# A token-major value projection in one pass of 512 columns over four PSUM banks

## The chip, the cores and the metric

The kernel runs on one core of one Trainium2 chip. Its engines work side by side, each through its own list of instructions in order: PE (TensorE, matmuls into PSUM; PEld is its weight load), DVE (VectorE), ACT (ScalarE), POOL (GpSimd) and SP (SyncE, which issues nearly all transfers). The metric is device time in microseconds (us) of one execution; lower is better. Before the change it is 1659.42 us, the median of 3 runs.

## The reference

Two layers of a decoder trunk over 512 tokens of width 2048, in float32. Each layer normalises its input, makes one wide projection of it, runs four mixers on slices of that (a gated linear attention GLA, a gated recurrence LRU, a sparse attention NSA and a convolution module, the Conformer), gates and merges them, and projects back:

```
def hybrid_layer(x, ...):
    h = rmsnorm(x, pre_g)
    proj = h @ w_in
    (gla_q, gla_k, gla_v, ..., conv_z) = jnp.split(proj, ...)
    o_a = gla_mixer(gla_q, gla_k, gla_v, ...)      # also lru, nsa, conformer
    mixed = jnp.concatenate([o_a, o_b, o_c, o_d], axis=-1)
    y = (group_rmsnorm(mixed, branch_g) * silu(z)) @ w_out
    return x + rmsnorm(y, post_g)
```

The change concerns gla_v alone: 512 tokens x 512 columns, a product over 2048 input features.

## The kernel before

Each float32 operand is split in two parts, hi and lo, of a shorter format; a product is three matmuls that add up in one PSUM bank (mm3, L198): hi x hi, hi x lo, lo x hi. The normalised input lies in SBUF as 16 feature tiles H[kk], L[kk] of 128 features x 512 tokens. Weights come in units of 128 x 1024 numbers (unit, L155): one transfer into a raw buffer (2 of them), then two splits of 512 columns each, hi by ACT (L144) and lo by DVE or POOL (L145), into whi and wlo (5 buffers each, N_W).

PSUM has eight banks of 128 x 512 float32. Four of them (pool acc) belong to the projections, three (mx) to the mixers' short products, one (op) to longer ones. Most projections (proj, L248) have the weights as stationary operand and fill one acc bank with 128 output columns x 512 tokens (tile pfm); the copy out of it, by `scaled` (L261) or a multiply, frees the bank. The value projection has tokens on the partitions instead: H is stationary and the weights move, so one bank holds 128 tokens, and four blocks of tokens b make the whole. It is done in two passes of 256 columns (loop hf): in each, two banks hold two blocks of tokens each, and for each of 16 feature tiles and each b three matmuls of 256 columns run. Eight units of weights serve a layer, four per pass. At the end of a pass ACT copies the four blocks into gv (L881). The tm projection (L795) before it is of the same kind, with four banks and 284 columns.

The mixers' work is a list of tasks, Python generators that emit a little at a time; `advance(budget)` runs them between projections, `flush` runs them out. The order that each engine gets is made from this by the tile scheduler at build time. It goes by priorities: matmuls of projections are in the band "last", so they fill PE where nothing else is ready, and loads, splits and copies of projections are in the band "first".

Around the value projection these are at work, in program order:
- `conformer_tail` (L365): the pointwise product pw_ps, then group_norm (L265) of four tiles: square (L270), split, a sum over channels in a bank gn_ps (chan_sum), root (ACT L204) and reciprocal (DVE L205), then a multiply that writes yconf.
- `compress` (L410): for each of kc and vc (tile kv) four units. A unit adds a position term to a slice of kv (L424), into one of the four slots of a ring, pbuf; splits that into zc (L426, L427); loads 128 x 1024 weights into mraw (one buffer), splits them into mhi and mlo (one buffer each, L144, L145), and adds 16 matmuls into the bank ch_ps. Behind the four units of kc, ACT copies ch_ps to the next ring slot (L438), and the matmul cf_ps reads it.
- `queries(0)` (L842) projects two NSA query heads before GLA's q and k (qk) are projected. Its two pfm banks are copied into q (L263).

Two lines say where kv and q lie: tiles with one tag share one buffer, so q can be written only after the last read of kv.

```
kvt = self.quad("t4", "kv")        # L826
qt = self.quad("t4", "q")          # L852
```

Of the kernel before, what the change touches and what calls it, by code (L numbers as in the profile page):

```python
# [13 lines left out]
AF = mybir.ActivationFunctionType  # L14
# [7 lines left out]
P = 128  # L22
KT = D // P
# [3 lines left out]
GLA_Q, GLA_K, GLA_V, GLA_FG, GLA_Z = 0, 256, 512, 1024, 1040  # L27
# [11 lines left out]
GV_UNIT = 8 + 2 * len(FM_TILES)  # L39
# [22 lines left out]
class Trunk:  # L62
# [649 lines left out]
    def layer(self, l, xs):  # L712
        nc, a, dve, act, gp = self.nc, self.a, self.dve, self.act, self.gp
        STEP = BUDGET
        STEP_N, STEP_Z = BUDGET_N, BUDGET_Z
# [8 lines left out]
        first = [self.bank(f"f{i}", self.acc, "acc") for i in range(4)]  # L724
# [7 lines left out]
        units = {}  # L732
        for u, t in steps:
# [7 lines left out]
            for k in (2 * u, 2 * u + 1):  # L741
                if l == 0:
                    self.put_h(H, L, k, self.x_of(xs, k), self.col(V_PRE + k))
                hi, lo = units[u][k % 2]
                with self.band("last"):
                    for i in range(4):
                        w = slice(i * P, (i + 1) * P)
                        self.mm3(first[i][:, tok], hi[:, w], lo[:, w], H[k][:, tok], L[k][:, tok],
                                 k == 0 and t == 0, k == KT - 1 and t == len(halves) - 1,
                                 skip_group_check=len(halves) > 1)  # L750
# [10 lines left out]
        rtok = self.rstd(sums, range(4), True)  # L761
# [34 lines left out]
        for kk in range(KT):  # L796
            if kk % 2 == 0:
                parts = self.unit(a["w_tm"][l, kk // 2], 2 * TM, TM)
            hi, lo = parts[kk % 2]
            with self.band("last"):  # L800
                for b in range(4):
                    tb = slice(b * P, (b + 1) * P)
# [9 lines left out]
        for b in range(4):  # L812
            with self.band("first"):
                act(tm[b], ptm[b][:, :TM], AF.Copy, scale=rtok[:, 2 * b:2 * b + 1])
            w = slice(b * 256, b * 256 + 256)
# [43 lines left out]
                    self.stt(qk[:, (2 * p + i) * 512:(2 * p + i + 1) * 512], ps, s, self.rbc, ALU.mult, ALU.mult)  # L859
                self.advance(STEP_N)  # L860
        gv = self.quad("t6", "gv")
        for hf in range(2):
            pv = [self.bank(f"gv{i}", self.acc, "acc") for i in range(2)]
            for u in range(4):
                parts = self.unit(a["w_in"][l, GV_UNIT + 4 * hf + u])
                with self.band("last"):
                    for k in range(4):
                        kk = 4 * u + k
                        hi, lo = parts[k // 2]
                        w = slice(k % 2 * 256, (k % 2 + 1) * 256)  # L870
                        for b in range(4):
                            tb = slice(b * P, (b + 1) * P)
                            o = pv[b // 2][:, (b % 2) * 256:(b % 2) * 256 + 256]
                            self.mm3(o, H[kk][:, tb], L[kk][:, tb], hi[:, w], lo[:, w],
                                     kk == 0 and b % 2 == 0, kk == KT - 1 and b % 2 == 1, skip_group_check=True)
                if u % 2 == 1:
                    self.advance(STEP_N)
            for i in range(2):
                for b in (2 * i, 2 * i + 1):
                    with self.band("first"):  # L880
                        act(gv[:, 512 * b + 256 * hf:512 * b + 256 * hf + 256],  # L881
                            pv[i][:, (b % 2) * 256:(b % 2) * 256 + 256], AF.Copy, scale=rtok[:, 2 * b:2 * b + 1])
        self.flush()
        queries(1, qt[:, 1024:])
        self.tasks.append(self.group_norm(NSA))
# [53 lines left out]
        o = [self.quad(f"t{i}", "o") for i in range(4)]  # L939
# [6 lines left out]
        H, L = self.nextH or (None, None)  # L946
# [25 lines left out]
def lay_out(x, pre_norm_g, w_in, gla_w_fg2, gla_b_fg2, lru_conv_w, lru_conv_b, lru_w_a, lru_b_a, lru_w_x, lru_b_x,  # L972
            lru_lambda, nsa_cmp_pos_k, nsa_cmp_w1_k, nsa_cmp_w2_k, nsa_cmp_pos_v, nsa_cmp_w1_v, nsa_cmp_w2_v,
            conf_dw_w, conf_dw_b, conf_ln_g, conf_ln_b, conf_pw_w, conf_pw_b, branch_norm_g, w_out, post_norm_g):
    n = DEPTH
    d = {}
    d["xT"] = np.ascontiguousarray(np.asarray(x)[0].T).reshape(4, 4, P, S).transpose(0, 2, 1, 3)
    w = np.asarray(w_in).reshape(n, KT, P, -1)

    def block(k0, k1, cols):  # L980
        b = w[:, k0:k1][..., cols]
        return b.transpose(0, 2, 1, 3).reshape(n, P, -1)

    units = []
    first = np.concatenate([np.arange(c, c + P) for c in FIRST4])
    for u in range(8):
        units.append(block(2 * u, 2 * u + 2, first))
    for c in FM_TILES:
        for h in range(2):
            units.append(block(8 * h, 8 * h + 8, np.arange(c, c + P)))  # L990
    for hf in range(2):
        for u in range(4):
            units.append(block(4 * u, 4 * u + 4, np.arange(GLA_V + 256 * hf, GLA_V + 256 * hf + 256)))
    d["w_in"] = np.stack(units, axis=1)
    tmc = np.concatenate([np.arange(NSA_VS, NSA_VS + P), np.arange(NSA_VW, NSA_VW + P),
                          np.arange(NSA_G, NSA_G + 12), np.arange(GLA_FG, GLA_FG + 16)])
    d["w_tm"] = np.stack([block(k, k + 2, tmc) for k in range(0, KT, 2)], axis=1)
    wo = np.asarray(w_out).reshape(n, KT, P, KT, P)[:, ORDER].reshape(n, 2, 8, P, KT, P)
    d["w_out"] = np.ascontiguousarray(wo.transpose(0, 4, 1, 3, 2, 5)).reshape(n, 2 * KT, P, 1024)

    def cols(t, m):
        return np.asarray(t).reshape(n, m, P).transpose(0, 2, 1)

    def taps(t):
        t = np.asarray(t)
        return t.reshape(n, t.shape[1], 4, P).transpose(0, 3, 2, 1).reshape(n, P, -1)

    d["vec"] = np.concatenate(
        [cols(pre_norm_g, 16), cols(post_norm_g, 16), cols(branch_norm_g, 16)[:, :, ORDER], taps(lru_conv_w), cols(lru_conv_b, 4),
         cols(lru_b_a, 4), cols(lru_b_x, 4), cols(lru_lambda, 4), taps(conf_dw_w), cols(conf_dw_b, 4),  # L1010
         cols(conf_ln_g, 4), cols(conf_ln_b, 4), cols(conf_pw_b, 4), cols(gla_b_fg2, 2)], axis=2)
    d["lru_w"] = np.concatenate([np.asarray(t).transpose(0, 2, 1, 3).reshape(n, P, 512) for t in (lru_w_a, lru_w_x)], axis=2)
    d["pw_w"] = np.asarray(conf_pw_w).reshape(n, 2, 2, P, 512).transpose(0, 1, 3, 2, 4).reshape(n, 2, P, 1024)
    d["w_fg2"] = np.repeat(np.pad(np.asarray(gla_w_fg2), ((0, 0), (0, 16), (0, 0)))[:, None], 3, axis=1).reshape(n, 96, 256)
    d["cmp_pos"] = np.concatenate([np.asarray(t).transpose(0, 2, 1) for t in (nsa_cmp_pos_k, nsa_cmp_pos_v)], axis=2)
    d["cmp_w2"] = np.concatenate([np.asarray(nsa_cmp_w2_k), np.asarray(nsa_cmp_w2_v)], axis=2)
    d["cmp_w1"] = np.stack([np.asarray(t).reshape(n, 4, 8, P, P).transpose(0, 1, 3, 2, 4).reshape(n, 4, P, 1024)
                            for t in (nsa_cmp_w1_k, nsa_cmp_w1_v)], axis=1)
    con = np.zeros((P, NCON), np.float32)
    i = np.arange(P)  # L1020
    con[:, C_ID:C_ID + P] = np.eye(P)
    con[:, C_TRI + 128:C_TRI + 256] = np.where(i[None, :] <= i[:, None], 0.0, NEG)
    t = np.arange(4)[None, :, None] * P + i[:, None, None]
    con[:, C_CMP:C_CMP + 124] = np.where(t >= 16 * np.arange(31)[None, None] + 31, 0.0, NEG).reshape(P, 124)
    con[:, C_GLA:C_GLA + P] = (i[:, None] // 64 == i[None] // 64) & (i[:, None] <= i[None])
    con[:62, C_FOLD:C_FOLD + 31] = np.concatenate([np.eye(31), np.eye(31)])
    d["consts"] = con
    return {k: np.ascontiguousarray(t) for k, t in d.items()}
# [18 lines left out]
```

## Time and profile before

| | |
|---|---|
| median of 3 runs | 1659.42 us (1657.36 to 1660.86) |
| the profiled execution | 1658.41 us, its span 1656.6 us |
| PE busy | 1600.3 us, 8380 matmuls |
| DVE / ACT / POOL busy | 1025.5 / 728.3 / 515.3 us |
| mean granted TensorE clock | 0.988 |
| value projection, layer 0 / 1 | starts at 301.26 / 1122.71 us |

The span runs from the first to the last instruction. Times within it count from its start. A matmul's duration reaches into the next one's, so the pace of PE is read from the starts. In a row of a timeline the bracket at the end is the idle time of that engine before the instruction and what ended it.

### The profile page before, as it was taken

The page shows a single profiled execution, that of the slowest core. Times are in us where ns is not written, and L with a number is a line of the kernel's source. Part 1 is how long each engine was busy: PE and PEld are TensorE (multiplying, and loading weights), DVE is VectorE, ACT ScalarE, POOL GpSimd, SP SyncE. Part 2 cuts the span into 40 slices and gives each one's busy share as a digit, 9 for nine tenths or more (in the row PEclk, how much of TensorE's full clock was granted, in tenths as well). Part 3 has the DMA queues.
Part 4 walks back from the last instruction along what each step waited for, and adds up shares of the span by engine and source line. Part 5 has one row for each costly group of instructions (what it writes and reads, how often), then busy time and mean ns, then how long its engine had stood idle before and what let it go on. Part 6 is the DMA issues. An engine that isn't in the chain of part 4 may idle for free.

```text
span 1656.6 us, 22323 instructions
## 1 busy us (share of the span) xinstructions
PE 1600.3 (97%) x8380; PEld 1356.3 (82%) x8380; DVE 1025.5 (62%) x1630; ACT 728.3 (44%) x1307; POOL 515.3 (31%) x431
## 2 busy tenths in 40 slices
PE   7999989999999998999999999999999999999996
PEld 6889878998888777888888898779988887778886
DVE  8488978554666758111396888876546757581115
ACT  6322463544456625333353234545444456353331
POOL 1354262121122422222245543521211234132224
PEclk9999999999999999999999999999999999999998
DMA  7322322242112223333343223222521121333323
GB/s 246 103 91 81 114 76 90 90 148 98 52 65 92 77 92 118 121 102 98 98 142 108 97 88 100 78 96 84 165 78 39 64 79 64 140 115 102 100 91 115
DMA packets 53708, 165.53 MB, mean 100 GB/s; under 512 B 5792, under 2 KB 14688, under 8 KB 52576
## 3 DMA queue, kind: packets, MB, share of 16 engines
q1 hardware_dynamic: 52224, 162.79, 29.9%
q8 instruction: 66, 1.08, 0.3%
q10 hardware_dynamic: 1376, 1.31, 0.2%
q14 instruction: 42, 0.34, 0.1%
HBM read 155.69 MB, written 8.39 MB: 99 GB/s over the span
## 4 chain that ended last, share of the span: by engine, by line
PE 81%; DVE 11%; ACT 4%; issue 3%; DMA 1%; POOL 0%; SPq 0%; DVEq 0%; ACTq 0%; POOLq 0%
PE pfm L196 39%; PE out_ps L196 19%; PE gv L196 6%; PE tm L196 3%; PE f L196 2%; PE o_ps L196 2%; DVE wlo L145 2%; PE s_ps L196 2%; PE pw_ps L196 1%; DVE L L131 1%; DVE gn_ps L205 1%; PE pt_ps L529 1%; PE go_ps L196 1%; PE ch_ps L196 1%; DVE o L691 1%
## 5 line engine op out<-in xcount | busy, mean ns | idle before, releaser
L144 ACT ACTIVATE whi<-raw 128x512 fp32r<-128x512 f32 (+1 forms) x512 | 313.0, 616 | 626.3 <-PE pfm L196 293.4
L145 POOL TENSOR_TENSOR wlo<-raw,whi 128x512 fp32r<-128x512 f32 (+1 forms) x229 | 294.0, 1285 | 836.2 <-ACT whi L144 755.0
L196 PE MATMUL pfm<-H,whi 128*128 128x512 f32 x1152 | 453.9, 394 | 0.0
L196 PE MATMUL pfm<-L,whi 128*128 128x512 f32 x1152 | 453.2, 393 | 0.0
L196 PE MATMUL pfm<-H,wlo 128*128 128x512 f32 x1152 | 452.5, 393 | 0.0
L145 DVE TENSOR_TENSOR wlo<-raw,whi 128x512 fp32r<-128x512 f32 x283 | 223.4, 794 | 322.1 <-ACT whi L144 320.9
L196 PEld LDWEIGHTS pfm<-H,whi 128*128 128x128 f32 x1152 | 217.6, 189 | 46.3 <-issue 1.2
L196 PEld LDWEIGHTS pfm<-H,wlo 128*128 128x128 f32 x1152 | 217.6, 189 | 45.4 <-issue 0.3
L196 PEld LDWEIGHTS pfm<-L,whi 128*128 128x128 f32 x1152 | 217.4, 189 | 45.5 <-issue 0.9
L196 PE MATMUL out_ps<-H,wlo 128*128 128x512 f32 (+1 forms) x576 | 211.3, 367 | 5.3 <-DVE wlo L145 5.3
L196 PE MATMUL out_ps<-L,whi 128*128 128x512 f32 (+1 forms) x576 | 210.9, 367 | 1.0 <-DVE L L233 1.0
L196 PE MATMUL out_ps<-H,whi 128*128 128x512 f32 (+1 forms) x576 | 209.8, 367 | 0.0
L131 DVE SCALAR_TENSOR_TENSOR cv_ps<-yv,vec,cv_ps 128x512 f32<-128x512 f32 x232 | 175.1, 755 | 7.2
L196 PEld LDWEIGHTS out_ps<-H,wlo 128*128 128x128 f32 x576 | 108.9, 189 | 24.0 <-DVE wlo L145 6.6
L196 PEld LDWEIGHTS out_ps<-L,whi 128*128 128x128 f32 x576 | 108.9, 189 | 20.0 <-DVE L L233 2.2
L196 PEld LDWEIGHTS out_ps<-H,whi 128*128 128x128 f32 x576 | 108.7, 189 | 17.5
L205 DVE RECIPROCAL gn_ps<-gn_ps 128x512 f32<-128x512 f32 x32 | 107.4, 3358 | 9.0 <-ACT gn_ps L204 9.0
L196 PE MATMUL gv<-whi,H 128*128 128x256 f32 x256 | 72.6, 284 | 0.7 <-ACT gv L881 0.7
L196 PE MATMUL gv<-wlo,H 128*128 128x256 f32 x256 | 72.5, 284 | 0.0
L196 PE MATMUL gv<-whi,L 128*128 128x256 f32 x256 | 72.3, 283 | 0.0
L196 PE MATMUL f<-H,whi 128*128 128x256 f32 (+1 forms) x192 | 57.0, 331 | 7.4 <-ACT whi L144 7.4
L196 PE MATMUL f<-L,whi 128*128 128x256 f32 (+1 forms) x192 | 60.2, 330 | 2.2 <-DVE L L131 2.2
(284 smaller groups left out, 2297.4 us busy)
## 6 DMA issues: line engine op xcount, KB each, us to landing
raw<-w_in SPq DMA_DIRECT2D x175, 512.0 KB, 3.2
raw<-w_out SPq DMA_DIRECT2D x64, 512.0 KB, 3.6
mraw<-cmp_w SPq DMA_DIRECT2D x16, 512.0 KB, 3.7
raw<-w_tm SPq DMA_DIRECT2D x16, 284.0 KB, 2.8
xs<-xT SPq DMA_DIRECT2D x16, 256.0 KB, 6.0
xs<-xT SPq DMA_DIRECT2D x4, 1024.0 KB, 4.8
x_scratch<-xs SPq DMA_DIRECT2D x16, 256.0 KB, 2.3
xs<-x_scratch SPq DMA_DIRECT2D x4, 1024.0 KB, 5.2
```

Source lines behind the costliest of these rows:

```text
L131: self.dve.scalar_tensor_tensor(out, in0, s, in1, op0=op0, op1=op1)
L144: self.act(hi, src, AF.Copy)
L145: eng.tensor_sub(lo, src, hi.bitcast(F32))
L196: self.nc.tensor.matmul(out, lhsT, rhs, start=start, stop=stop, **kw)
L205: self.dve.reciprocal(out, out)
L529: self.tr(pt[:, (2 * j + h) * P:(2 * j + h + 1) * P], pb[h][br][:, (j0 + j) * P:(j0 + j + 1) * P], ident)
L691: e[0].tensor_mul(ov, ov, (r if e[0] is dve else rs)[:, None, :].to_broadcast([P, k1 - k0, n]))
```

## The change

The two passes become one. Four acc banks are taken at once, one per block of tokens, and each matmul moves 512 columns, so a layer has 192 matmuls where it had 384. A unit of weights now holds two feature tiles x 512 columns, not four x 256; there are eight units as before. Four copies of 512 columns replace eight of 256 in a layer. The tasks are advanced four times, as before.

```
-        for hf in range(2):
-            pv = [self.bank(f"gv{i}", self.acc, "acc") for i in range(2)]
-            for u in range(4):
-                parts = self.unit(a["w_in"][l, GV_UNIT + 4 * hf + u])
...
-                            o = pv[b // 2][:, (b % 2) * 256:(b % 2) * 256 + 256]
-                            self.mm3(o, H[kk][:, tb], L[kk][:, tb], hi[:, w], lo[:, w],
-                                     kk == 0 and b % 2 == 0, kk == KT - 1 and b % 2 == 1, skip_group_check=True)
-                if u % 2 == 1:
-                    self.advance(STEP_N)
...
+        pv = [self.bank(f"gv{b}", self.acc, "acc") for b in range(4)]
+        for kk in range(KT):
+            if kk % 2 == 0:
+                parts = self.unit(a["w_in"][l, GV_UNIT + kk // 2])
+            hi, lo = parts[kk % 2]
+            with self.band("last"):
+                for b in range(4):
+                    tb = slice(b * P, (b + 1) * P)
+                    self.mm3(pv[b], H[kk][:, tb], L[kk][:, tb], hi, lo, kk == 0, kk == KT - 1)
+            if kk % 4 == 3:
+                self.advance(STEP_N)
+        for b in range(4):
+            with self.band("first"):
+                act(gv[:, 512 * b:512 * b + 512], pv[b], AF.Copy, scale=rtok[:, 2 * b:2 * b + 1])
...
-    for hf in range(2):
-        for u in range(4):
-            units.append(block(4 * u, 4 * u + 4, np.arange(GLA_V + 256 * hf, GLA_V + 256 * hf + 256)))
+    for u in range(8):
+        units.append(block(2 * u, 2 * u + 2, np.arange(GLA_V, GLA_V + 512)))
```

The scheduler puts the instructions in another order from there on. In the lists, gv0 to gv3 are the projection's banks and the number behind a name tells one buffer from another; gn_ps_2146 to 2182 are the four sums of the Conformer's norm, ch_ps_2273 belongs to kc and ch_ps_2452 to vc. On PE, layer 0, this stands before at the first sum of that norm:

```order
L196 MATMUL gv0_3042<-whi_3104,L5_223 128x256
L196 MATMUL gv1_3043<-whi_3104,H5_222 128x256
L196 MATMUL gn_ps_2146<-shi_2142,ones_85 128x512
L196 MATMUL gv1_3043<-wlo_3105,H5_222 128x256
L196 MATMUL gv1_3043<-whi_3104,L5_223 128x256
L196 MATMUL gv1_3043<-whi_3104,H5_222 128x256
```

The same place on PE now:

```order
L196 MATMUL gv1_3043<-whi_3185,H4_206 128x512
L196 MATMUL gv1_3043<-wlo_3186,H4_206 128x512
L196 MATMUL gv1_3043<-whi_3185,L4_207 128x512
L196 MATMUL gn_ps_2146<-shi_2142,ones_85 128x512
L196 MATMUL gn_ps_2146<-slo_2143,ones_85 128x512
L196 MATMUL gn_ps_2158<-shi_2154,ones_85 128x512
L196 MATMUL gn_ps_2158<-slo_2155,ones_85 128x512
L196 MATMUL gn_ps_2170<-shi_2166,ones_85 128x512
L196 MATMUL gn_ps_2170<-slo_2167,ones_85 128x512
L196 MATMUL gn_ps_2182<-shi_2178,ones_85 128x512
L196 MATMUL gn_ps_2182<-slo_2179,ones_85 128x512
L196 MATMUL ch_ps_2273<-mhi_2280,zc_2275 62x128
```

Before, 6 to 12 matmuls of gv stood between two of gn (76 ahead of the last two), and 42 to 61 between two units of ch. Now the eight gn and the 64 ch of kc stand together, behind the first 30 matmuls of gv0 and gv1, with no other matmul among them. Where the units of kc end, PE had this before:

```order
L196 MATMUL gv1_3400<-wlo_3629,H15_442 128x256
L196 MATMUL gv1_3400<-whi_3628,L15_443 128x256
L196 MATMUL gv1_3400<-whi_3628,H15_442 128x256
L196 MATMUL cf_ps_2272<-consts_82,pbuf_2188 128x31
L196 MATMUL gv1_3400<-wlo_3629,H15_442 128x256
L196 MATMUL gv1_3400<-whi_3628,L15_443 128x256
L196 MATMUL ch_ps_2452<-mhi_2459,zc_2454 62x128
```

and has this now:

```order
L196 MATMUL ch_ps_2273<-mlo_2431,zc_2425 31x128
L196 MATMUL ch_ps_2273<-mhi_2430,zc_2425 62x128
L196 MATMUL cf_ps_2272<-consts_82,pbuf_2188 128x31
L196 MATMUL ch_ps_2452<-mhi_2459,zc_2454 62x128
L196 MATMUL gv2_3044<-whi_3048,H0_118 128x512
L196 MATMUL gv2_3044<-wlo_3049,H0_118 128x512
L196 MATMUL gv2_3044<-whi_3048,L0_119 128x512
```

Before, cf stood at the end of the value projection. Now the third bank, gv2, begins behind cf. On DVE, layer 0, the copies out of the two banks of queries(0), pfm_2195 and pfm_2352, stood here before:

```order
L145 TENSOR_TENSOR mlo_2460<-mraw_2457,mhi_2459 128x1024
L145 TENSOR_TENSOR wlo_3730<-raw_3723,whi_3729 128x512
L424 TENSOR_TENSOR pbuf_2188<-kv_1657,pos_2267 128x248
L263 TENSOR_TENSOR q_2190<-pfm_2195,rbc_519 128x512
L263 TENSOR_TENSOR q_2190<-pfm_2352,rbc_519 128x512
```

and stand here now:

```order
L145 TENSOR_TENSOR mlo_2333<-mraw_2330,mhi_2332 128x1024
L145 TENSOR_TENSOR mlo_2431<-mraw_2428,mhi_2430 128x1024
L424 TENSOR_TENSOR pbuf_2188<-kv_1657,pos_2267 128x248
L263 TENSOR_TENSOR q_2190<-pfm_2195,rbc_519 128x512
L263 TENSOR_TENSOR q_2190<-pfm_2352,rbc_519 128x512
L145 TENSOR_TENSOR mlo_2460<-mraw_2457,mhi_2459 128x1024
```

They follow the eighth add on kv in both. On DVE and ACT the weight splits of the value projection from the sixth feature tile on now stand behind these copies, and on SP its loads from the ninth on stand behind five or more of the unit loads into mraw. Ahead of the copies the norm's and the units' instructions stand nearly as they did, without the splits between them. Layer 1 has the same pattern.

## Rows read from the trace of the kernel before

**Rows 1.** Page, part 1: busy us (share of the span) xinstructions.
```profile
PE 1600.3 (97%) x8380; PEld 1356.3 (82%) x8380; DVE 1025.5 (62%) x1630; ACT 728.3 (44%) x1307; POOL 515.3 (31%) x431
```
**Rows 2.** Page, part 5: group | busy, mean ns | idle before, releaser.
```profile
L196 PE MATMUL gv<-whi,H 128*128 128x256 f32 x256 | 72.6, 284 | 0.7 <-ACT gv L881 0.7
```
**Rows 3.** Timeline of PE, layer 0: start us, us, instruction; 42nd pfm, 22nd gv.
```profile
284.76 0.39 PE L196 MATMUL pfm<-H,whi 128*128 128x512 f32 x1
...
294.05 0.39 PE L196 MATMUL pfm<-H,wlo 128*128 128x512 f32 x1
...
301.26 0.28 PE L196 MATMUL gv<-whi,H 128*128 128x256 f32 x1
...
303.77 0.28 PE L196 MATMUL gv<-whi,H 128*128 128x256 f32 x1
```
**Rows 4.** Chain that ended last, 300 to 365: start us, us, what.
```profile
306.75 3.73 PE pw_ps L196 x16
...
335.19 0.97 PE ch_ps L196 x16
...
359.40 0.34 PE cf_ps L196 x2
```
**Rows 5.** Timeline of DVE, layer 0.
```profile
323.01 3.35 DVE L205 RECIPROCAL gn_ps<-gn_ps 128x512 f32<-128x512 f32 x1
326.27 0.67 DVE L145 TENSOR_TENSOR wlo<-raw,whi 128x512 fp32r<-128x512 f32 x1
326.86 0.40 DVE L427 TENSOR_TENSOR zc<-pbuf,zc 128x248 fp32r<-128x248 f32 x1
...
327.84 3.36 DVE L205 RECIPROCAL gn_ps<-gn_ps 128x512 f32<-128x512 f32 x1
...
337.86 1.49 DVE L424 TENSOR_TENSOR pbuf<-kv,pos 128x248 f32<-128x248 f32 x3
...
351.66 1.23 DVE L145 TENSOR_TENSOR mlo<-mraw,mhi 128x1024 fp32r<-128x1024 f32 x1 [1.23 <-ACT mhi L144]
357.88 1.23 DVE L145 TENSOR_TENSOR mlo<-mraw,mhi 128x1024 fp32r<-128x1024 f32 x1 [4.99 <-ACT mhi L144]
...
359.77 0.59 DVE L424 TENSOR_TENSOR pbuf<-kv,pos 128x248 f32<-128x248 f32 x1
360.39 1.29 DVE L263 TENSOR_TENSOR q<-pfm,rbc 128x512 f32<-128x512 f32 x2
```
**Rows 6.** Timeline of ACT, layer 0.
```profile
315.28 0.63 ACT L270 ACTIVATE sq<-yconf 128x512 f32<-128x512 f32 x1 [0.27 <-PE gn_ps L196]
...
317.16 1.28 ACT L204 ACT_TABLE_LOAD   x1
318.45 0.66 ACT L204 ACTIVATE gn_ps<-gn_ps,eps 128x512 f32<-128x512 f32 x1
```
**Rows 7.** Timelines of PE and of ACT, layer 1.
```profile
1122.71 0.28 PE L196 MATMUL gv<-whi,H 128*128 128x256 f32 x1
...
1136.03 0.63 ACT L270 ACTIVATE sq<-yconf 128x512 f32<-128x512 f32 x1 [0.63 <-PE gn_ps L196]
```
**Rows 8.** Page, part 6: transfer, issuer, count, KB, us to landing.
```profile
mraw<-cmp_w SPq DMA_DIRECT2D x16, 512.0 KB, 3.7
```
**Rows 9.** Timeline of PE near the start.
```profile
29.32 1.22 PE L196 MATMUL f<-H,wlo 128*128 128x512 f32 x4 [2.08 <-DVE wlo L145]
```
**Rows 10.** Stretches: busy us (x), then PEclk, DMA share, GB/s.
```profile
30.36:33.76 3.40, 3.40 (x10) 2.62 (x9) 3.40 (x7) 0.20 (x2) 1.68 (x5) 0.50 0.49 154
...
146.00:158.00 12.00, 12.00 (x92) 12.00 (x91) 11.43 (x16) 2.90 (x7) 6.00 (x8) 1.00 0.24 62
```
**Rows 11.** Waits of PE: who waited for whom, us in total, times, longest.
```profile
PE out_ps L196 <- DVE wlo L145: 5.3, 3, 3.7
...
PE o_ps L196 <- ACT pth L534: 1.8, 2, 0.9
```

More of the change, by code (lines that the diff above doesn't have):

```diff
@@ L861, in layer @@
         gv = self.quad("t6", "gv")
-        for hf in range(2):
-            pv = [self.bank(f"gv{i}", self.acc, "acc") for i in range(2)]
-            for u in range(4):
-                parts = self.unit(a["w_in"][l, GV_UNIT + 4 * hf + u])
[L866 to L872, printed above, removed]
-                            o = pv[b // 2][:, (b % 2) * 256:(b % 2) * 256 + 256]
-                            self.mm3(o, H[kk][:, tb], L[kk][:, tb], hi[:, w], lo[:, w],
-                                     kk == 0 and b % 2 == 0, kk == KT - 1 and b % 2 == 1, skip_group_check=True)
-                if u % 2 == 1:
-                    self.advance(STEP_N)
[L878 to L882, printed above, removed]
+        pv = [self.bank(f"gv{b}", self.acc, "acc") for b in range(4)]
[12 more added lines that the diff above has]
+                act(gv[:, 512 * b:512 * b + 512], pv[b], AF.Copy, scale=rtok[:, 2 * b:2 * b + 1])
         self.flush()
```

## The prediction

> **What bounds the kernel now.** I read the page's busy line first: PE is busy for 97% of the span [rows 1]. So work taken from PE, or idle time given to it, reaches the end almost one to one, and the other engines count only where PE must wait for them. Second, the costliest groups: the value projection is 3 x 256 matmuls of 256 columns, and one of its three groups shows an idle 0.7 us released by ACT's copy of gv [rows 2]. The reader should stop there: with four acc banks the second pass should not need the banks of the first. It did, so two of the four banks were held by something else.
>
> Third, the DVE timeline of layer 0 says by what. The two q copies of queries(0) run at 360.39, right behind an add that reads kv, at 359.77 [rows 5]. They empty the two banks that queries(0) filled before the q/k projections of GLA, and they write tile t4, which is kv's until the compress task has made its last read of it. That eighth add writes a slot of a ring of four, whose former content the matmul cf reads, the first step behind the four units of kc. So two acc banks stay full until four of the eight compress units have gone through PE. The old projection lived in the other two banks, two per pass. The new one wants four.
>
> **The change part by part.** *Fewer matmuls.* Spacing between starts: 512 columns (294.05 - 284.76) / 41 = 0.2266 us, 256 columns (303.77 - 301.26) / 21 = 0.1195 us [rows 3]. Per layer 384 x 0.1195 - 192 x 0.2266 = 45.9 - 43.5 = 2.4 us less, 4.8 in both. The rows thus charge about 12.5 ns per matmul beside the columns. The Trainium skill (TensorE: Matmul & The Clock Gate, "Wait — 56ns, not 53.3ns?") gives a fixed floor of some 2.5 ns per warm matmul. By it the estimated gain would be 1.0 us for the 384 that go, and the sum below 3.8 us higher, 1729; the trace disagrees, and I take the rows.
>
> *Evictions and loads.* ACT's 16 copies become 8 wider ones; DVE, POOL and SP split and load the same 8 units of weights per layer. The evictions stand beside PE work, except that the projection after gv needs a bank: nine matmuls (2 us) follow the last one of gv0, against one copy of under 0.8 us, so I take 0 (0 to 0.8 per layer).
>
> *The new wait on PE.* In the new order PE does 30 matmuls of gv0 and gv1, 24 of pw, the 8 of gn, 64 of ch, cf and one more ch, and only then the first of gv2, which needs the first q copy. What stands behind it on PE is everything: it takes matmuls as they stand, and the splits of later weights wait too, since the five whi buffers are held until gv2 and gv3 have read the first units. So I walk the chain to gv2 in layer 0.
>
> - PE arrives: 301.26 + 30 x 0.2266 + 24 x 0.233 (3.73 / 16) = 313.7 [rows 3, 4]. The last pw matmul ends 1.1 later than now, since 512 columns stand ahead of it.
> - The conformer norm: the third square (now 315.28, tied to the first gn sum) comes at about 315.1; then only table load and root follow: 0.63 + 1.28 + 0.66, so the first reciprocal starts at 317.7 [rows 6].
> - DVE then has, in the new order, 4 reciprocals, 3 yconf multiplies, 2 slo, 4 zc, 3 adds (one merged row) and the lo half of compress unit 2. From start to start a reciprocal takes 326.27 - 323.01 = 3.26, a split 0.59, a zc with a multiply behind it 327.84 - 326.86 = 0.98; the three adds take 1.4 (1.49 with overlap), a lo half 1.23 [rows 5]. 4 x 3.26 + 2 x 0.59 + 3 x 0.98 + 0.4 + 1.4 + 1.2 = 20.2, so unit 2's lo half ends at 337.9. DVE takes them in order, so no faster norm helps.
> - Each further unit is load, hi, lo through one raw buffer: 357.88 - 351.66 = 6.2 us a round [rows 5]. Two rounds bring the lo half of unit 4 to 350.3. Behind it ch, the copy, cf, the add and the first q copy end at about 353.5. But the single ch in front of gv2 belongs to unit 5, and needs its load (3.7 [rows 8]) and hi half (6.2 - 1.2 - 3.7, some 1.2 with the hand-over): 355.2. That is the later one, and gv2 starts there.
>
> PE is held from 313.7 to 355.2, 41.5 us. In it it does work that it did before too: 8 gn of 512 columns, 65 ch at 0.97 / 16 each and cf at 0.34 / 2 [rows 4], together 1.8 + 3.9 + 0.2 = 5.9. New idle time: 35.6 us.
>
> In layer 1 gv starts at 1122.71, so PE arrives at 1135.1; the third square is tied to the gn sum there (1136.03 now) and comes at about 1135.5, right behind the first gn matmul, as against 1.4 us behind it in layer 0 [rows 7]. The rest is the same list: 1138.1, 1158.3, 1170.7, 1175.6. Held 40.5, idle 34.6 us.
>
> *The clock.* After a wait of 2.08 us that ended at 29.32 the granted clock was 0.50 from 30.36 to 33.76, that is the 1.2 GHz level, and then full again [rows 9, 10]. I expect the same after each long hold: half of 3.4, so 1.7 us a layer. Bounds: 0, and the whole rest of gv at the lower level, 162 matmuls of 0.2266 us doubled, 36.7 us a layer; I stay at the row. Within the hold the ch matmuls may be slow too; at twice 0.97 us they still hide behind DVE and the loads, except ch ahead of cf, which has 1.6 us to spare.
>
> *Afterwards.* The compress units 5 to 8 now run inside gv, no longer inside queries(1), so attend starts with some 144 more matmuls of projections left as cover. Four groups of PE waits lie in the stages behind gv (out_ps, ds and two of o_ps), from 5.3 down to 1.8 us, some 13 in all [rows 11]. Bounds of what comes back: 0 to 13; I take 2, as most of it is single short waits.
>
> Sum: 35.6 + 34.6 + 3.4 - 4.8 - 2 = 66.8. The profiled execution took 1658.41 us (span 1656.6), 1.0 below the median of 1659.42 and inside the spread of the three runs, so I add it as it is: 1658.4 + 66.8 = 1725.2, called 1725.
>
> **The rivals.** *Only the narrower instruction count shows (faster).* If the q copies ran before PE reaches gv2, nothing would be held and the time would be 1658.4 - 4.8 = 1653.6. It decides at 313.7 in layer 0. For it: kv's first four reads are done early, and without the weight splits DVE and ACT are free sooner. Against it: the copies come at 360.39 now, and four reciprocals and three loads in a row, some 37 us by rows, stand between. 3%.
>
> *The hold is paid back later.* The tasks behind gv start no later than now by the clock, and PE has some 33 us more projection work to put between their steps; if all of the 13 us vanish, 1714. Against it: single waits there are short, and most belong to stages that the change doesn't reach. 12%.
>
> *The clock stays low.* Four banks in turn, three matmuls each, could keep the clock moving between its levels. All of the rest of gv at 1.2 GHz costs 2 x 36.7 - 3.4 = 70 more: 1795. Against it: the tm projection turns through four banks in the same way, three matmuls at a time, and its stretch shows a granted clock of 1.00 [rows 10]. This is the case of the Trainium skill's "A second HAM failure mode: psum-queue depth-cycling" (TensorE: Matmul & The Clock Gate), where short waits between groups on changing banks make the clock swing; by the tm row the trace does not show it here. 3%.
>
> **How the numbers follow.** The forecast, held in both layers with short recovery, has 82%: 1725, itself good for 12 or so either way, since each round of loading may take 5.9 to 7 us (three rounds twice, 6 us) and the start of the norm may slip by 1 or 2 a layer. The paid-back case pulls the low end to 1703, with 10 us to spare for a hold shorter by 5 a layer. The high end, 1746, takes slower rounds, a second short hold per layer and the clock's level lasting twice as long. The measurement can tell about 0.2% (3.3 us) from no change. Faster: the first rival, 0.03. Same: what lies between it and a hold almost fully hidden, 0.02. Slower: 0.95.
>
> **What would show it.** Right: one idle stretch of PE per layer, in pieces, 33 to 37 us in sum, between gv1 and gv2, its last piece released by mhi or by the q copy on DVE; the q copies in layer 0 near 353 and not 360; gv from about 301 to 398; a PEclk of 0.5 just behind the hold; gv matmuls 0.227 apart else. Wrong: PE without idle time of over 5 us there, which would mean that the third bank was free; or idle time as forecast and a total below 1700, which would put the cover of later stages at more than I gave it.

## The result and the profile after

The changed kernel takes 1706.08 us (median of 4 runs, 1705.08 to 1712.21), the one before 1658.83 beside it: 1.0292 times as long (95% interval 1.0277 to 1.0308), 47 us slower. The direction and the mechanism came as forecast; the size was 19 us under 1725. The profiled execution took 1705.67 us with a span of 1703.9, and the lines below are its own.

The page, parts 1 and 2 (busy us with the share of the span; busy tenths in 40 slices; granted clock in tenths):
```profile
PE 1603.9 (94%) x7996; PEld 1341.5 (79%) x7996; DVE 1023.5 (60%) x1630; ACT 729.4 (43%) x1299; POOL 511.9 (30%) x431
...
PE   8999989589999999999989999994999999999996
...
PEclk9999999789999999999999999996899999999998
```
PE has 384 matmuls fewer than in [rows 1] and is busy 3.6 us longer, with two dents, one per layer. Where they are, the timeline of PE tells (start us, us, instruction, idle time ahead and releaser), in layer 0 and then in layer 1:
```profile
312.16 0.40 PE L196 MATMUL gn_ps<-shi,ones 128*128 128x512 f32 x1
...
352.60 0.36 PE L196 MATMUL ch_ps<-mhi,zc 128*62 128x128 f32 x1 [1.69 <-ACT mhi L144]
352.76 0.73 PE L196 MATMUL gv<-whi,H 128*128 128x512 f32 x1
353.29 0.63 PE L196 MATMUL gv<-wlo,H 128*128 128x512 f32 x1
...
356.61 0.40 PE L196 MATMUL gv<-whi,H 128*128 128x512 f32 x1
...
1197.38 0.37 PE L196 MATMUL ch_ps<-mhi,zc 128*62 128x128 f32 x1 [1.79 <-ACT mhi L144]
1197.55 0.74 PE L196 MATMUL gv<-whi,H 128*128 128x512 f32 x1
```
Between gv1 and gv2 nothing of the projection runs for 40.6 us, from 312.16 to 352.76. The matmul in front of gv2 is the single ch of unit 5, released by the hi half, as the prediction said. The waits of PE from 300 to 400 us (who waited for whom, us, times, longest) give the pieces:
```profile
PE ch_ps L196 <- DVE mlo L145: 12.9, 3, 5.0
PE ch_ps L196 <- DVE yconf L131: 3.9, 1, 3.9
PE gn_ps L196 <- DVE slo L145: 3.6, 3, 2.6
PE gn_ps L196 <- DVE yconf L131: 3.1, 1, 3.1
PE gn_ps L196 <- ACT shi L144: 1.8, 1, 1.8
PE ch_ps L196 <- ACT mhi L144: 1.7, 1, 1.7
PE cf_ps L196 <- ACT pbuf L438: 0.4, 1, 0.4
```
They sum to 27.4 us (27.7 in layer 1), less than the 35 that the hold costs and than the 33 to 37 that the prediction named as its sign: inside it PE runs its 75 matmuls, nearly all of them at the lower clock, so they fill 13 us and not the 5.9 that they took before. A reader who counts only idle time misses that part. The windows show the clock (busy us of PE, PEld, DVE, ACT, POOL, then PEclk, DMA share, GB/s):
```profile
316.00:330.00 14.00, 3.58 (x11) 1.88 (x12) 13.80 (x12) 5.24 (x11) 0.00 (x0) 0.50 0.00 0
330.00:353.00 23.00, 8.01 (x64) 7.12 (x63) 12.43 (x16) 6.20 (x10) 0.42 (x1) 0.50 0.22 71
352.76:356.48 3.72, 3.72 (x10) 2.95 (x11) 2.64 (x3) 1.12 (x3) 3.04 (x2) 0.50 0.39 122
356.20:399.50 43.30, 43.30 (x239) 35.73 (x237) 11.39 (x15) 17.90 (x30) 6.95 (x7) 1.00 0.37 129
1197.55:1203.00 5.45, 5.45 (x14) 4.29 (x15) 2.53 (x2) 1.12 (x3) 3.01 (x2) 0.50 0.32 99
```
DVE is full in the first window (the reciprocals) and half idle in the second (the loads). And the chain on DVE, which answers to [rows 5]:
```profile
316.20 3.37 DVE L205 RECIPROCAL gn_ps<-gn_ps 128x512 f32<-128x512 f32 x1 [1.80 <-ACT gn_ps L204]
...
335.02 1.21 DVE L145 TENSOR_TENSOR mlo<-mraw,mhi 128x1024 fp32r<-128x1024 f32 x1
...
346.72 1.22 DVE L145 TENSOR_TENSOR mlo<-mraw,mhi 128x1024 fp32r<-128x1024 f32 x1 [4.66 <-ACT mhi L144]
350.95 0.57 DVE L424 TENSOR_TENSOR pbuf<-kv,pos 128x248 f32<-128x248 f32 x1 [3.00 <-PE cf_ps L196]
351.55 1.29 DVE L263 TENSOR_TENSOR q<-pfm,rbc 128x512 f32<-128x512 f32 x2
```
The eighth add waits for cf, and the q copies follow it at once.

Now the stages. Each stretch runs from the first matmul of a kind to that of the next, in us (gv is the value projection, out the output projection with its bank out_ps), in the profiled executions. Those of runs 1, 2, 6 and 10 took 3.5 to 5.8 us more than the medians of these runs. (The kernels with queries(0) behind gv are left out, since other work lies in their stretches.)

| kernel | gv to out, layer 0 | out to gv of layer 1 | gv to out, layer 1 | out to the end |
|---|---|---|---|---|
| before | 336.4 | 485.0 | 337.6 | 196.3 |
| changed | 367.0 | 478.5 | 365.8 | 192.8 |
| 1: one pass, no hold | 334.3 | 485.0 | 344.4 | 195.7 |
| 2: old gv, q moved | 337.4 | 484.9 | 337.6 | 197.8 |
| 3: old matmuls, four banks | 357.9 | 478.0 | 360.2 | 192.8 |
| 5: old gv, L on POOL | 336.3 | 487.1 | 340.8 | 195.7 |
| 6: changed, L on POOL | 367.2 | 481.4 | 370.5 | 193.7 |
| 8: changed, eight slots | 355.2 | 477.7 | 356.9 | 192.8 |
| 9: old gv, second raw | 340.0 | 479.0 | 336.1 | 196.5 |
| 10: run 1, second raw | 339.7 | 478.5 | 344.4 | 195.8 |
| 12: changed, second raw | 362.4 | 477.5 | 360.5 | 192.8 |

The projection's stretches grow by 30.6 and 28.2 us; the two that hold the output projections shrink by 6.5 and 3.5, though the change doesn't touch them; and gv of layer 0 starts 1.5 us earlier. That makes the 47.3 us between the spans. The 1.5 us are no work of the change: the stretch at the lower clock from 30.36 us on [rows 10] is missing in this execution, behind a wait of 1.89 us in the place where it was 2.08:
```profile
28.00:36.00 8.00, 6.67 (x29) 5.55 (x30) 8.00 (x14) 3.73 (x8) 2.63 (x6) 1.00 0.26 73
```

### The profile page after: what moved, and what is told of

It reads as the page before. It is cut to its first block, busy times and chain, and to the rows that moved or that the text cites. A ratio compares the mean times of both kernels' runs of the same rounds, so it can differ in the third digit from the quotient of the medians.

```text
span 1703.9 us, 21534 instructions
## 1 busy us (share of the span) xinstructions
PE 1603.9 (94%) x7996; PEld 1341.5 (79%) x7996; DVE 1023.5 (60%) x1630; ACT 729.4 (43%) x1299; POOL 511.9 (30%) x431
## 4 chain that ended last, share of the span: by engine, by line
PE 80%; DVE 9%; issue 4%; ACT 3%; DMA 3%; POOL 1%; SPq 0%; DVEq 0%; ACTq 0%; POOLq 0%
PE pfm L196 39%; PE out_ps L196 20%; PE gv L196 5%; PE tm L196 3%; PE f L196 2%; PE o_ps L196 2%; PE s_ps L196 2%; DMA mraw<-cmp_w 1%; DVE L L131 1%; PE pw_ps L196 1%; DVE wlo L145 1%; PE go_ps L196 1%; PE pt_ps L529 1%; PE ds_ps L196 1%; DVE gn_ps L205 1%
## 5 line engine op out<-in xcount | busy, mean ns | idle before, releaser
L196 PE MATMUL f<-H,wlo 128*128 128x256 f32 (+1 forms) x192 | 53.8, 327 | 4.0 <-DVE wlo L145 4.0
L196 PE MATMUL gv<-wlo,H 128*128 128x512 f32 x128 | 52.4, 409 | 0.0
L145 DVE TENSOR_TENSOR mlo<-mraw,mhi 128x1024 fp32r<-128x1024 f32 x22 | 26.9, 1222 | 42.1 <-ACT mhi L144 42.1
```

What stands on the lines that cost most here:

```text
L145: eng.tensor_sub(lo, src, hi.bitcast(F32))
L196: self.nc.tensor.matmul(out, lhsT, rhs, start=start, stop=stop, **kw)
```

## The experiments

**1. Is it the hold?** The q rows go over the halves of kv, so that the first two copies wait for no read of compress; one pass of 512 stays.
```diff
-        qt = self.quad("t4", "q")
-        queries(0, qt)
+        qt = kvt
+        queries(0, qt[:, 1024:])
...
-        queries(1, qt[:, 1024:])
+        queries(1, qt[:, :1024])
```
Expected: 

> One pass of 512 columns as in the changed kernel, but the q rows of queries(0) are written over the upper half of kv (its K halves, read early) and those of queries(1) over the lower half, so that the first two q copies no longer wait for the compress task's reads. Theory (the loss is the hold of two acc banks): no idle stretch of PE inside gv, gv ends near 360 us in layer 0 and not near 397, the out_ps waits of the old kernel (5.3 us) are back since there is no hold to pay them, and the time is 1658.8 - 4.8 = 1654 us (1650 to 1660). Rival (512 columns through four banks in turn are slow in themselves, by clock or by eviction): still 1690 us or more.

Measured: 1659.82 us, 1.0016 (1.0006 to 1.0026). PE waits nowhere from 300 to 400 us, and gv runs at the full clock (window, columns as above):
```profile
302.00:355.30 53.30, 53.30 (x257) 43.87 (x256) 34.99 (x39) 28.18 (x48) 6.95 (x6) 1.00 0.32 101
```
So the loss is the hold, and not the width. But the 4.8 us did not come. In layer 1 this kernel waits in attend where the old one did not (pct_ps, among its waits; out_ps is back, too). It runs at the lower clock behind that wait, and once more behind one for ds_ps of 2.39 us, which the old kernel has too (2.35 us), there without a stretch at the lower clock (its waits, then windows with columns as above):
```profile
PE out_ps L196 <- DVE wlo L145: 6.0, 2, 3.7
...
PE pct_ps L553 <- DVE st L514: 3.0, 1, 3.0
```
```profile
1265.00:1277.00 12.00, 10.40 (x49) 9.15 (x50) 7.51 (x25) 6.25 (x15) 0.00 (x0) 0.57 0.01 1
1404.00:1413.00 9.00, 6.74 (x16) 4.89 (x17) 7.91 (x9) 3.36 (x7) 9.00 (x8) 0.62 0.05 11
```
12 x 0.43 + 9 x 0.38 = 8.6 us of time at full clock are lost there, against 1.7 in that stretch of before. With 2.6 us more idle time (8.0 against 5.4) and 2.4 less for the matmuls that makes nearly the 6.8 us by which the stretch grew (8.6 - 1.7 + 2.6 - 2.4 = 7.1). The profiled execution is 3.7 us above the run's median, so some of this is its own.

**2. The same edit alone**, on the old projection. Expected: 

> The old projection (two passes of 256 columns), with the same new places of the q rows as in the run before; a control of the edit itself. Theory (the two held banks did not bound the old projection): 1658.8 us within 4, since only the 0.7 us of waits for the gv copies can go. Rival (the earlier q rows are what makes the one-pass version of the run before fast, whatever the width): as much faster here, 1654 us or less.

Measured: 1657.05 us, 0.9995 (0.9986 to 1.0003), no change. The held banks cost the old kernel nothing that can be measured.

**3. Width or banks?** The old matmuls, with the two passes interleaved and all copies behind the last of them:
```diff
-        for hf in range(2):
-            pv = [self.bank(f"gv{i}", self.acc, "acc") for i in range(2)]
-            for u in range(4):
+        pv = [[self.bank(f"gv{i}", self.acc, "acc") for i in range(2)] for hf in range(2)]
+        for u in range(4):
+            for hf in range(2):
...
```
Expected: 

> The old 256-column matmuls, same weights and same number, but the two passes interleaved unit by unit, so that four acc banks are wanted at once; the q rows stay where they are. 144 gv matmuls (17.2 us) stand ahead of the first one on the third bank. Theory (demand of four banks, not the width): the third bank comes at about 353 us in layer 0 as in the changed kernel, so 53.1 - 28.7 = 24.4 us of idle time a layer, 48.8 in all, plus 3.4 of low clock, less some 14 to 18 that the stages behind give back: 1694 us (1685 to 1705), with no out_ps wait over 1 us. Rival (it is the width of 512, whole banks written by one block): 1659 us within 5.

Measured: 1691.91 us, 1.0203 (1.0190 to 1.0216). The third bank comes 55.4 us behind the start of gv (53.1 in the changed kernel), on PE's timeline:
```profile
353.72 0.63 PE L196 MATMUL cf_ps<-consts,pbuf 62*128 62x31 f32 x2 [0.36 <-ACT pbuf L438]
356.36 0.53 PE L196 MATMUL gv<-whi,H 128*128 128x256 f32 x1
```
The demand of four banks does it, with matmuls of 256 columns as well. The hold itself is shorter than expected, 17.0 and 17.9 us with 3.3 of work in it; in layer 0 PE waits another 5.0 us in gv for splits of weights.

**4. queries(0) behind gv**, in the changed kernel.
```diff
-        qt = self.quad("t4", "q")
-        queries(0, qt)
         qk = self.quad("t5", "qk")
...
         self.flush()
+        qt = self.quad("t4", "q")
+        queries(0, qt)
         queries(1, qt[:, 1024:])
```
Expected: 

> One pass of 512 columns, with the four projections of queries(0) (192 matmuls) moved behind gv, so that no bank waits for a q copy while gv runs; kv and q keep their shared tile. Theory: no hold in gv, but the first attend task starts later and has less projection work as cover behind it: 1654 to 1668 us. Rival (the q copies then hold two banks of the queries(1) or z projections instead, and PE stands there): 1680 us or more, with idle time of PE ahead of pfm released by the q copy or by mlo.

Measured: 1657.42 us, 0.9989 (0.9980 to 0.9998). No hold, and no other in its place; again next to nothing of the 4.8 us shows.

**5 to 7. The waits in front of the output projection.** Half of the L steps go to POOL:
```diff
-            self.dve.tensor_sub(lo, src, h.bitcast(F32))
+            (self.gp if k % 2 else self.dve).tensor_sub(lo, src, h.bitcast(F32))
```
The old kernel. Expected: 

> The old kernel, with every second low half L in front of the output projection (line 233) computed on POOL and not on DVE, 8 of 16 a layer. PE waits 3.7 and 0.6 us there in layer 0, 1.6 and 0.4 in layer 1, behind a DVE that works without a pause, and runs at a lower clock for a few us behind the longest wait. Theory (these waits with their clock are what the changed kernel gets back): the old kernel gains them, 4.3 + 1.7 in layer 0 and 2.0 + 0.5 in layer 1, that is 8.5 us: 1650 us (1648 to 1655). Rival (the gain in the stages behind comes from something else, and the new POOL steps of about 1.28 us only make another wait): 1657 to 1662.

Measured: 1661.22 us, 1.0012 (1.0002 to 1.0021). The changed one. Expected: 

> The changed kernel with the same edit of L. Theory (its hold already gave these waits back, none is left at out_ps): no gain, 1706 us within 2. Rival (the edit is a gain of its own, whatever the hold): as much faster as the old kernel, 1698 us or so.

Measured: 1709.58 us, 1.0312 (1.0292 to 1.0332). The kernel of run 4. Expected: 

> One pass of 512 columns, queries(0) behind gv, and the edit of L. Theory (without a hold the 4.8 us of fewer matmuls come back as waits for DVE at out_ps, and the edit frees both): 1657.4 - 8.5 = 1649 us, down to 1645 if the fewer matmuls show as well. Rival (something else takes the 4.8 us, or the edit only makes POOL late): 1654 us or more.

Measured: 1657.40 us, 0.9990 (0.9981 to 0.9999). Runs 5 and 7 miss their theories: the old kernel with the edit still waits at the start of the output projection (630 to 830 us).
```profile
PE out_ps L196 <- DVE wlo L145: 3.2, 1, 3.2
...
PE out_ps L196 <- ACT whi L144: 1.4, 1, 1.4
```
The split that PE waits for stands on DVE behind the last reciprocal of GLA's norm, not behind the L steps; taking these off DVE frees nothing. Run 6 gained nothing either (it waits 1.4 us for a split on POOL there), so these three don't tell the theories on the gain apart.

**8. A shorter hold.** The ring of compress in eight slots of 256 (and back to four of 512 at the start of attend):
```diff
-        self.ring, self.pi = [pbuf[:, i * 512:(i + 1) * 512] for i in range(4)], 0
+        self.pbuf, self.ring, self.pi = pbuf, [pbuf[:, i * 256:(i + 1) * 256] for i in range(8)], 0
...
```
Expected: 

> The changed kernel, with the compress task's ring cut into eight slots of 256 and not four of 512, so that its eighth add no longer waits for cf, and the q copies come behind the fourth reciprocal of the conformer norm: about 334.5 us in layer 0 in place of 352, gv2 18.5 us a layer earlier. The hold left is 34.2 - 18.5 and 33.4 - 18.5, 30.6 us in all. Theory (the stages behind gv give back a fixed 18.6 us, fewer matmuls and low clock counted in, as soon as the hold is longer than that): 1658.2 + 30.6 - 18.6 = 1670 us (1666 to 1674). Rival (they give back in proportion to the hold, some 9): 1680 us. Rival (the hold does not hang on that ring): 1706.

Measured: 1685.58 us, 1.0163 (1.0148 to 1.0179). PE's timeline, layer 0:
```profile
336.25 0.80 PE L196 MATMUL gv<-whi,H 128*128 128x512 f32 x1 [3.94 <-DVE q L263]
```
The ring is the link: the third bank comes 35.5 us behind the start of gv, released by the q copy itself. My sum was 16 us short. 48 ch and cf (3.2 us a layer) now follow the hold, and the bank came 0.9 later than I wrote, 8 us in all. The rest is the gain: the output stretches gave their 7.3 and 3.5 as with the long hold, those of attend and GLA next to nothing (18.8 us more in layer 0, where hold, clock and matmuls make 20.2 + 1.5 - 2.4). So it is not one fixed sum. A share of the hold it may be by the totals (11.5 of 40.5 us here, 19.6 of 68.6 in the changed kernel, 28% and 29%), but not by the stages, of which the output stretches give the same with either hold.

**9 to 11. The same gain without a hold?** Every second load of compress goes to a free half of pbuf (the ring keeps four slots of 256):
```diff
-                hi, lo = self.mixer_unit(a["cmp_w1"][l, i, u])
+                hi, lo = self.mixer_unit(a["cmp_w1"][l, i, u], self.pbuf[:, 1024:] if u % 2 else None)
...
```
The old kernel. Expected: 

> The old kernel; only the compress task is changed: its loads go by turns into mraw and into half of pbuf (whose ring keeps four slots of 256), so that a load no longer waits for the split before it. A round of a unit, 5.9 us with its load of 3.4, should fall to about 4, so compress ends some 13 us earlier and with it the tasks behind (attend, GLA, its norm). Theory (the two output stages are 7.0 and 3.5 us shorter in every kernel with a hold because the tasks end earlier against PE there, whatever the cause): 1658.5 - 10.5 = 1648 us, out_ps waits gone, with no hold and no change of gv. Rival (the hold does it by something else, or the tasks don't move): 1656 to 1660.

Measured: 1654.70 us, 0.9977 (0.9965 to 0.9988). The kernel of run 1. Expected: 

> One pass of 512 columns without a hold (the q rows over the halves of kv), with the second place for the loads of compress. Theory: the 1659.8 us of that kernel less 10.5, and the waits of attend in layer 1 (pct_ps, 3.0) gone as well: 1646 to 1650 us. Rival: 1657 to 1661.

Measured: 1654.12 us, 0.9978 (0.9967 to 0.9989). The kernel of run 4. Expected: 

> One pass of 512 columns, queries(0) behind gv, with the second place for the loads of compress. Theory: 1657.4 - 10.5 = 1647 us. Rival: 1655 to 1659.

Measured: 1653.12 us, 0.9968 (0.9957 to 0.9978), the one that beats both kernels by most. All three gain, by a third to a half of what I expected. The first step of the theory failed: in the old kernel compress ends no earlier, since the last lo half starts at 379.2 us (379.37 before). The last step came true in layer 0 alone. There the last reciprocal of GLA's norm ends 4.4 us behind the start of the output projection in all three, where it was 12.4 before, and of 4.3 us of out_ps waits 0.5 is left (run 9, 630 to 830 us):
```profile
PE out_ps L197 <- DVE wlo L145: 0.5, 1, 0.5
```
With the lower clock behind them (1.7 and 3.4 us less lost in runs 9 and 10) these waits make nearly all of the 6.0 and 6.5 us by which the stretch of the first output projection shrinks in the table. The stretch ahead of it grows by 3.6 and 5.4, with 1.7 and 5.1 us more lost at the lower clock in these executions. In layer 1 the reciprocal still ends 10.9 us behind, and waits of 2.0 to 2.3 us stay. What brings the norm forward in layer 0 is not shown.

**12. The last links of the hold.** The edit of run 9 on the changed kernel. Expected: 

> The changed kernel with the second place for the loads of compress, to test the last links of the hold's chain: load 3.4, hi half 1.06, lo half 1.24, one after the other for units 3 to 5. Theory: behind the lo half of unit 2 (336.2 in layer 0) a round is hi, lo and ch, 1.06 + 1.24 + 1.7 + 0.1 of hand-over = 4.1 us in place of 5.9; unit 4's lo half ends at 344.4, and since the order now sets the whole ch of unit 5 ahead of the third bank, that bank starts near 350.3 and not 353: 3.6 us a layer less with the ch that no longer follows, some 1700 us (1696 to 1703). Rival (the loads are not what paces the hold): third bank at 353 or later, 1706 us or more.

Measured: 1695.15 us, 1.0231 (1.0208 to 1.0255). The chain of waits, layer 0:
```profile
342.95 1.24 DVE mlo L145
344.19 0.04 issue
344.23 1.93 PE ch_ps L197 x16
...
348.93 1.81 PE ch_ps L197 x15
350.74 6.09 PE gv L197 x24
```
No load is left in it, the rounds take 4.3 us, and gv2 starts 51.5 us behind the start of gv, 1.5 earlier than in the changed kernel. The time fell by more than expected: gv is back at its full pace at 351.87, 1.3 us behind the bank (2.1 in layer 1), where the changed kernel took 3.7 and 5.4. More ch stands just ahead of the bank here; whether that is the reason is not shown.

## Why the prediction was right, and where it was not

*The hold, step by step.* In us behind the start of gv, forecast and measured in layer 0: PE arrives 12.4 and 12.4, the third square 13.8 and 13.9, the first reciprocal 16.4 and 16.5, the end of unit 2's lo half 36.6 and 36.5, that of unit 4 49.0 and 48.2, gv2 53.9 and 53.05. Layer 1: 12.4 and 12.4, 12.8 and 12.9, 15.4 and 15.5, 35.6 and 35.5, 48.0 and 47.4, 52.9 and 52.3. Only the rounds of the loads were too long, 5.9 us where I took 6.2 from [rows 5], a round beside other traffic and splits. Runs 1 to 3, 8 and 12 show each link: the shared tile, the four banks, the ring and cf, the loads.

*The clock behind the hold.* Forecast 1.7 us a layer, from the 3.4 us of [rows 10]; measured 3.7 us at 0.50 in layer 0 (352.76 to 356.48) and 5.4 in layer 1 (1197.55 to 1203.00), so 1.9 and 2.7. Then the projection through four banks in turn keeps 1.00, as the window from 356.20 shows. That was the third rival's case, and run 1 with full clock through its whole gv of layer 0 excludes it a second time. The short waits on changing banks, by which the Trainium skill (TensorE: Matmul & The Clock Gate, "A second HAM failure mode: psum-queue depth-cycling") would have the clock swing, are not in this stretch; its trace neither confirms nor refutes the rule.

*Fewer matmuls.* The gain is there, in gv itself. Added up over both layers from the start of each gv matmul to the next start on PE, without waits and without what the lower clock costs, gv took 93.3 us before, 88.7 in the changed kernel, 87.9 in run 1 and 87.5 in run 4: 4.6 to 5.8 us less, 4.8 forecast. Yet runs 1 and 4 show that without a hold the total hardly gains by it. In run 1 idle time grew by 2.9 us and the loss at the lower clock by 5.0; in both, attend's small products pt_ps took 1.6 us longer. The rest of run 4's loss lies in no single place.

*Afterwards: the step that failed.* I took 2 us as given back, within 0 to 13. With the hold at 34.7 and 33.9, the clock at 4.6, the matmuls at -4.8 and the start at -1.5, the 47.3 us leave 19.6 us given back. So the choice of 2 was wrong, and the bound too. Of the four groups of waits, 13.4 us, both of [rows 11] are gone after, and of the other two 3.4 us are left (before, then after):
```profile
PE ds_ps L196 <- ACT gklt L626: 3.9, 2, 2.4
PE o_ps L196 <- DVE ptl L535: 2.4, 2, 1.2
```
```profile
PE ds_ps L196 <- ACT gklt L626: 2.6, 2, 2.1
PE o_ps L196 <- DVE ptl L535: 0.8, 1, 0.8
```
These waits, which I called single and short, went nearly whole, 10.0 us of them. And the bound of 13 counted idle time only. I had charged 1.7 us of low clock to each hold that the change adds, and none to the waits that it takes away. Before, these stretches stood behind the waits (windows, columns as above):
```profile
579.60:583.00 3.40, 3.40 (x9) 2.48 (x8) 3.35 (x5) 0.74 (x2) 3.40 (x5) 0.54 0.45 154
651.70:655.10 3.40, 3.40 (x10) 2.67 (x9) 2.08 (x4) 2.61 (x2) 0.70 (x1) 0.52 0.68 183
1268.80:1273.00 4.20, 3.42 (x16) 3.42 (x17) 2.17 (x5) 0.82 (x2) 1.25 (x1) 0.59 0.02 4
```
They cost 3.4 x 0.46 + 3.4 x 0.48 + 4.2 x 0.41 = 4.9 us, and none of the three is left after. The last eight matmuls of the program, rs and rb of the closing norm, take 1.32 us in place of 1.99, since the clock falls between them before and behind both after: 0.7. With 11.2 us of idle time less in all (1.5 and 3.4 from gv to the output projections, 4.3 and 2.0 at out_ps) that is 16.8 of the 19.6; 2.8 I can't place. The 4.9 us are what these two executions show and no price of each wait: the stretch of [rows 10] and the one behind ds_ps in run 1 stand behind waits that are as long, to 0.2 us, in another execution without a stretch at the lower clock.

Why the waits went: the tasks run on while PE stands. Counted from the start of gv in layer 0, attend starts (cs_ps) after 99.5 us before and 99.6 after, and the last reciprocal of GLA's norm ends after 348.8 and 345.2; the output projection starts after 336.4 and 367.0. So that reciprocal ends 12.4 us behind the start of the output projection before; after, it ends 22 us ahead of it (the row of DVE before, then the chain of waits and the row of DVE after):
```profile
646.73 3.35 DVE L205 RECIPROCAL gn_ps<-gn_ps 128x512 f32<-128x512 f32 x1
```
```profile
639.22 27.70 PE pfm L196 x122
666.91 13.15 PE out_ps L196 x58
```
```profile
638.36 6.56 DVE L205 RECIPROCAL gn_ps<-gn_ps 128x512 f32<-128x512 f32 x2
```
The order on PE, which is made at build time, has the same in it: between the last sum of that norm and the first out_ps stand 7 matmuls of projections in layer 0 and 9 in layer 1 before, 122 and 126 after, and no out_ps waits. The other kernels agree, on single profiles. Where 38 or more stand there (runs 3, 8 and 12) out_ps does not wait; in run 6, with 122 and 126, only for the splits on POOL. With 7 and 9 (runs 1, 2, 4, 5 and 7) the waits are 4.2 to 5.0 and 1.5 to 2.3 us; with 24 and 9 (runs 9 to 11) 0.5 us and 2.0 to 2.3. The tasks' own times are not the same in all of them: attend starts after 89 us in runs 3 and 12, after 104 in run 8. What the kernels with a hold share is the cover.

This is the second rival's mechanism, to which I gave 12% and 1714 us; the result lies nearer to it than to my forecast. Against it I said that these waits belong to stages that the change doesn't reach. The table above says otherwise: with four kernels that hold banks (changed, 3, 8 and 12) the stretches of the output are 477.5 to 478.5 and 192.8 us, with before and runs 1 and 2, 484.9 to 485.0 and 195.7 to 197.8. Runs 9 and 10 have 479.0 and 478.5 in layer 0 without a hold, so it takes no hold to lose these waits. A stage whose waits are set by tasks that run beside PE is reached by whatever moves PE against them.

## What to carry to other kernels

Before a pass takes more banks, list who holds the others at that moment, and follow the release to its end, here through a shared tile, a ring and a matmul to four loads. Where side tasks run beside a bound engine, a stall early on is partly paid for by the waits that it makes needless later: count those, and the stretches at the lower clock that the profile shows behind them. A gain of 0.3% in matmuls can drown in one or two such stretches, so ask what PE will wait for next before booking it.

## What was not expected of the hardware

In the hold PE is busy a third of the time, at a granted clock of 0.50, and 16 ch matmuls take 1.93 us at that clock (run 12's chain) against 0.97 in [rows 4]. How long the lower clock lasted behind it differed: 3.7 us in layer 0, 5.4 in layer 1; 1.3 and 2.1 us in run 12, where 32 ch and cf ran in the 6 us ahead of the bank; 3.0 in run 8, where PE had stood for 3.9 us just ahead. And of two waits of 2.35 and 2.39 us in the same place (ds_ps, layer 1) one was followed by the lower clock and one was not. What decides it no run here shows.
